# A delta-net scan kept in two halves of one PSUM bank, its output products in the attention's ring

## The chip, the cores and the metric

The kernel runs on one core of a Trainium2 chip. The metric is the device time of one execution in microseconds. Its engines are TensorE (PE, with its weight loads as PEld), VectorE (DVE), ScalarE (ACT), GpSimd (POOL) and SyncE (SP, which here only issues DMAs).

## The reference

Two layers act on 1280 tokens (256 of context, 1024 latent). Each layer normalises and modulates its input, multiplies it by one wide input weight, sends the parts through three branches, and adds the gated product with one output weight to the residual. A final norm follows. The branches are a gated delta net (GDN, 4 heads of 64), multi-head latent attention (8 heads), and gated linear attention (GLA, 4 heads). GDN and GLA are scanned in both directions, by chunks:

```
def step(state, xs):                       # gated delta net, one chunk of 64
    v_new = ui - wi @ state
    o = (qi * exp(gi)) @ state + ai @ v_new
    state = state * exp(g_last) + (ki * exp(g_last - gi)).T @ v_new
```

The GLA scan has the same form without the first line: `o = (qi * exp(bi)) @ state + scores @ vi` and a decayed state plus `k.T @ v`. The output is the normed latent stream, 1024 x 1024 in float32. The second layer needs no output for context tokens.

## The kernel before

A layer runs in stages that `run` (L1419) strings together: input projections and convolution, preparation of the delta net's triangular inverses, the up-projection of attention (`up`), attention itself (`attend`), and the output projection (`proj_start`, `proj`). Beside `up` and `attend` runs a **background**, a Python generator that gives out instructions piece by piece: the delta net's scan (`gdn_scan`, L683), then the GLA preparation and its seven levels, then the GLA scan (`gla_scan`, L926). After each unit of `up` the background gets three turns, until 28 have been taken in all (`UPS`); after each piece of `attend` it gets one turn. What is left when attention has been given out is drained, and then comes `proj_start`.

This order of the program gives the priorities. At compile time a planner simulates the engines, and of the instructions that are ready in its simulation it places the one that comes first in the program; each engine then runs its list strictly in the order so made. A lower instruction can thus stand ahead of a higher one that was not ready.

PSUM has eight banks of 128 x 512 float32. One (`tag="l"`, one buffer) belongs to the background for the whole of `up` and `attend`. The other seven are the ring "u" during `up`; during `attend` they are two score tiles `sa` of two banks each, one bank `sb`, and the ring "t" of **two** banks, from which attention takes one tile for each group of four transposes of the probabilities (`ptr`, L1243, copied out at L1247) and one for each output (`O`, L1255 to L1271). A new tile of a ring waits until every access of the tile that it replaces is over. Two engines' accesses to one bank are kept apart even where they touch different columns.

**One step of the delta net's scan** (20 in a layer, both directions and four heads at once; `S` is the state) takes three tiles of bank "l" in turn:

- `kS` (L730): the key products with S into columns 0 to 255 and, where the step has an output, the query products into 256 to 511. DVE forms `r` from the left half (L732, L733) and `qs` from the right (L736). Then a turn ends.
- `Tr` (L740): the products of the triangular inverse with `r`; DVE makes `vn` (L742). A turn ends.
- `F` (L748, L759): the state's product in the left half, which DVE adds to the decayed state to make the next S (`Sg`, L754; the decay `sd` is POOL's, L753); and the intra-chunk product of `at` with `vn` in the right half, which DVE adds to `qs` to give the output `oS` (L762). After steps 3, 15 and 19 POOL adds the two directions (L774) and `head_norm` gates them and stores them. A turn ends.

In the first layer every step has an output, in the second those from step 4 on. All float32 matmuls count as two records in the trace.

**One step of the GLA scan** (10) takes three tiles of the same bank: `kdt` (L950, two transposes of keys, copied by ACT to `ktl` at L952), `gO` (L961, L964: products with the state and with the scores, taken out by L973 or L975) and `gF` (L980, from which DVE makes the next state, L982 and L988). Each of the three ends a turn.

`proj_start` (L1296) loads attention's results (`yst`, L1316), splits the first output weights, makes gate rows (L1331, L1332) and turns the gated GDN and GLA results (`ytr`, L1350, from `yx`, L1346). Its SBUF pool is opened when the background's pools have been closed. `proj` goes on with `ytr` and the products `po` (L255 to L257).

Of the kernel before, what the change touches and what calls it, by code (L numbers as in the profile page):

```python
# [43 lines left out]
class Net:  # L44
# [638 lines left out]
    def gdn_scan(self, l):  # L683
# [8 lines left out]
        S = None  # L692
# [7 lines left out]

        for s in range(20):
# [3 lines left out]
            def kq(m, d, h):  # L705
                return self.KQ[h % 2].rearrange("q (m p i t) -> q m p i t", m=2, p=2, t=64)[R[d], m, h // 2, cc[d] // 2]
# [5 lines left out]
            def be(m):  # L712
# [13 lines left out]
            if S is not None:  # L726
                pk = self.g("kS", "l")
                for m in range(2 if out else 1):
                    for d, h in lanes:
                        mm(pk[R[d], 256 * m + 64 * h:256 * m + 64 * h + 64], kq(m, d, h), S[R[d], hs(h)], start=True, stop=True)  # L730
                r = sp.tile([128, 256], F32, name="r", tag="r", bufs=1)
                V.tensor_tensor(v3(r), v3(pk[:, 0:256]), be(3), ALU.mult)  # L732
                V.tensor_tensor(r, vt, r, ALU.subtract)  # L733
                if out:
                    qs = sp.tile([128, 256], F32, name="qs", tag="qs", bufs=1)
                    V.tensor_tensor(v3(qs), v3(pk[:, 256:512]), be(3), ALU.mult)  # L736
                yield
            pt = self.g("Tr", "l")
            for d, h in lanes:
                mm(pt[R[d], hs(h)], ci(self.TT, d, h), r[R[d], hs(h)], start=True, stop=True)  # L740
            vn = sp.tile([128, 256], F32, name="vn", tag="vn", bufs=1)
            V.tensor_tensor(v3(vn), v3(pt[:, 0:256]), be(0), ALU.mult)  # L742
            yield
            pf = self.g("F", "l")
            if s < 19:
                P.tensor_tensor(v3(kt), v3(kt), be(1), ALU.mult)
                for d, h in lanes:
                    mm(pf[R[1 - d], hs(h)], kt[R[d], hs(h)], vn[R[d], hs(h)], start=True, stop=True)  # L748
                Sn = sp.tile([128, 256], F32, name="Sg", tag="Sg", bufs=2)
                if S is not None:  # L750
# [3 lines left out]
                    V.tensor_tensor(Sn, sd, pf[:, 0:256], ALU.add)  # L754
                else:
                    V.tensor_copy(Sn, pf[:, 0:256])
            if out:
                for d, h in lanes:
                    mm(pf[R[d], 256 + 64 * h:256 + 64 * h + 64], at[R[d], h % 2, 64 * (h // 2):64 * (h // 2) + 64], vn[R[d], hs(h)], start=True, stop=True)  # L759
                o = oS[:, 256 * s:256 * s + 256]  # L760
                if S is not None:
                    V.tensor_tensor(o, qs, pf[:, 256:512], ALU.add)  # L762
                else:
                    V.tensor_copy(o, pf[:, 256:512])
            S = Sn
            for j in {3: (0,), 15: (2, 3), 19: (1, 4)}.get(s, ()):
# [817 lines left out]
```

## Time and profile before

| | |
|---|---|
| three runs, median (lowest to highest) | 2283.36 us (2278.01 to 2290.98) |
| the profiled execution's own time | 2280.18 us |
| its span, first to last instruction | 2278.4 us |
| PE busy | 2043.3 us, 90% |
| PE weight loads busy | 1709.8 us, 75% |
| DVE / ACT / POOL busy | 1291.6 (57%) / 941.1 (41%) / 743.7 (33%) us |
| mean granted TensorE clock | 0.946 |

Stages by time in the profile: the first layer's up-projection with the scan 499 to 618 us, a joint with little PE work to 646, attention with the scan to 781, with the GLA levels to 954, with the GLA scan to 1052, attention's rest to 1076, then the output projection. In the second layer the scan beside attention lasts from 1773 to 1907, the GLA scan from 2043 to 2137, attention's rest to 2171.

How to read it: a row names the engine, the line of the kernel, the operation, and out<-in by tile. In the timeline `[x <-y]` after a row is idle time of that engine just before it and what ended it. A row of a stage gives its bounds and length, then busy us and instructions of PE, PEld, DVE, ACT and POOL, then the granted share of TensorE's full clock, the busy share of the DMA engines and GB/s. Busy time of PE includes the overlap of pipelined matmuls, so a busy PE is not PE at its peak.

### The profile page before, as it was taken

How to read it: one execution, taken by the hardware profiler on the slowest of the kernel's cores; microseconds unless marked ns; L12 is line 12 of the kernel's file. 1: busy time of each engine (PE TensorE's matmuls, PEld its weight loads, DVE VectorE, ACT ScalarE, POOL GpSimd, SP SyncE). 2: the span in 40 equal slices, each digit the busy share in tenths (PEclk: the TensorE clock that was granted, in tenths of full speed). 3: DMA queues.
4: the chain of work that ended last, by engine and by line, in shares of the span. 5: the costliest groups of instructions: out<-in, count | busy, mean ns of one | idle time of the engine just before them, and what ended most of it. 6: DMA issues, size and time to landing. Idle time of an engine off the chain costs nothing.

```text
span 2278.4 us, 44490 instructions
## 1 busy us (share of the span) xinstructions
PE 2043.3 (90%) x17820; PEld 1709.8 (75%) x17820; DVE 1291.6 (57%) x2187; ACT 941.1 (41%) x1926; POOL 743.7 (33%) x936
## 2 busy tenths in 40 slices
PE   5998997999989988898897998976987999899998
PEld 3987896886767766676897987875876776667688
DVE  3446685323447689656425356795233677975634
ACT  3246311533235466555204356212542445564531
POOL 1233265122234543214103322381123264421410
PEclk8999998899989999999898999998998999899999
DMA  7111343258742231113424212424266242101352
GB/s 296 47 62 61 105 119 113 84 200 284 220 109 76 76 111 36 40 48 121 161 93 171 65 36 81 136 69 115 90 197 168 58 115 96 54 24 50 100 155 103
DMA packets 207551, 247.34 MB, mean 109 GB/s; under 512 B 60976, under 2 KB 164464, under 8 KB 203760
## 3 DMA queue, kind: packets, MB, share of 16 engines
q1 hardware_dynamic: 207344, 244.49, 34.1%
q8 instruction: 140, 2.29, 0.4%
q14 instruction: 67, 0.55, 0.1%
HBM read 168.14 MB, written 76.28 MB: 107 GB/s over the span
## 4 chain that ended last, share of the span: by engine, by line
PE 46%; DVE 13%; ACT 5%; DMA 5%; issue 3%; POOL 2%; SPq 1%; DVEq 0%; POOLq 0%; ACTq 0%
PE O L1255 6%; PE ptr L1243 4%; PE po L257 3%; PE po L255 3%; PE po L256 3%; PE sa L255 3%; PE sa L256 2%; PE sa L257 2%; PE ptk L255 1%; PE ptk L256 1%; PE ptk L257 1%; DVE XT L634 1%; DVE X L636 1%; PE kS L730 1%; DVE acc L345 1%
## 5 line engine op out<-in xcount | busy, mean ns | idle before, releaser
L255 PE MATMUL ptk<-whi,hhi 128*128 128x256 f32 (+1 forms) x912 | 263.6, 290 | 6.1 <-DVE ev L297 2.2
L257 PE MATMUL ptk<-whi,hlo 128*128 128x256 f32 (+1 forms) x912 | 261.9, 288 | 1.8 <-POOL hlo L238 1.7
L256 PE MATMUL ptk<-wlo,hhi 128*128 128x256 f32 (+1 forms) x912 | 261.7, 287 | 0.4 <-DVE wlo L250 0.4
L1243 PE MATMUL ptr<-c_id,P 128*128 128x128 f32 x1312 | 203.6, 283 | 27.8 <-ACT PT L1247 18.8
L1243 PEld LDWEIGHTS ptr<-c_id,P 128*128 128x128 f32 x1312 | 151.2, 143 | 78.1 <-ACT PT L1247 29.9
L1247 ACT COPY PT<-ptr 128x512 f32<-128x512 f32 (+1 forms) x256 | 122.3, 480 | 211.1 <-PE ptr L1243 209.7
L256 PE MATMUL pin<-hlo,whi 128*128 128x512 f32 (+1 forms) x544 | 201.6, 371 | 1.6 <-issue 1.6
L255 PE MATMUL pin<-hhi,whi 128*128 128x512 f32 (+1 forms) x544 | 202.5, 372 | 0.0
L257 PE MATMUL pin<-hhi,wlo 128*128 128x512 f32 (+1 forms) x544 | 201.8, 372 | 0.0
L255 PEld LDWEIGHTS ptk<-whi,hhi 128*128 128x128 f32 x912 | 179.4, 197 | 10.8 <-issue 4.3
L1206 DVE TENSOR_REDUCE mx<-sa 128x1 f32<-128x1024 f32 x128 | 156.2, 1220 | 53.6 <-PE sa L257 53.0
L257 PEld LDWEIGHTS ptk<-whi,hlo 128*128 128x128 f32 x912 | 178.8, 197 | 5.3 <-POOL hlo L238 3.0
L256 PEld LDWEIGHTS ptk<-wlo,hhi 128*128 128x128 f32 x912 | 179.4, 197 | 3.1 <-issue 2.0
L1255 PE MATMUL O<-PT,vv 128*64 128x256 f32 x1312 | 169.6, 388 | 1.7 <-ACT PT L1247 0.9
L255 PE MATMUL po<-wohi,yh 128*128 128x256 f32 x576 | 164.4, 286 | 4.4 <-DVE yl L1353 2.1
L256 PE MATMUL po<-wolo,yh 128*128 128x256 f32 x576 | 164.0, 285 | 0.0
L257 PE MATMUL po<-wohi,yl 128*128 128x256 f32 x576 | 162.6, 285 | 0.0
L1228 ACT ACTIVATE P<-sa,mx 128x1024 f32<-128x1024 f32 x128 | 142.2, 1111 | 0.0
L1255 PEld LDWEIGHTS O<-PT,vv 128*64 128x64 f32 x1312 | 97.2, 138 | 59.0 <-issue 11.9
L255 PE MATMUL sa<-kTh,qTh 128*128 128x512 f32 (+1 forms) x272 | 118.3, 436 | 21.1 <-ACT kTh L1152 15.2
L250 POOL TENSOR_TENSOR wlo<-wst,whi 128x1024 fp32r<-128x1024 f32 x32 | 84.1, 2639 | 127.5 <-ACT whi L249 126.4
L256 PEld LDWEIGHTS pin<-hlo,whi 128*128 128x128 f32 x544 | 105.6, 194 | 19.7 <-issue 4.4
(341 smaller groups left out, 5030.6 us busy)
## 6 DMA issues: line engine op xcount, KB each, us to landing
wada<-in_w_ada_dram SPq DMA_DIRECT2D x24, 1024.0 KB
wst<-in_w_in_dram SPq DMA_DIRECT2D x48, 512.0 KB
kv<-ktv_d SPq DMA_DIRECT2D x80, 128.0 KB
wost<-in_w_out_dram SPq DMA_DIRECT2D x16, 512.0 KB
xt<-in_x_all_dram SPq DMA_DIRECT2D x10, 512.0 KB
at_d<-D SPq DMA_DIRECT2D x4, 1280.0 KB
kn_d<-uo SPq DMA_DIRECT2D x20, 256.0 KB
v_d<-uo SPq DMA_DIRECT2D x20, 256.0 KB
```

The costliest lines, as they stand in the source:

```text
L250: E.tensor_tensor(lo[:, h], st, hi[:, h].bitcast(F32), ALU.subtract)
L255: mm(out, lh, rh, start=first, stop=False)
L256: mm(out, lh, rl, start=False, stop=False)
L257: mm(out, ll, rh, start=False, stop=last)
L345: nc.vector.scalar_tensor_tensor(a, raw[:, tap:tap + 1282], cw[:, ti, tap:tap + 1], a, ALU.mult, ALU.add)
L634: E.tensor_tensor(tmp, Xv[B, G, 0:k, k].unsqueeze(3).broadcast_to([q, n, nr, ncl]), Xv[B, G, k, k + 1:32].unsqueeze(2).broadcast_to([q, n, ...
L636: E.tensor_tensor(dst, dst, tmp, ALU.add)
L1206: V.tensor_reduce(mx[:, 0:1], sas[u], AX.X, ALU.max, negate=True)
L1228: A.activation(p[:, 0:1024], ta, AF.Exp, bias=mx[:, 0:1], accum_out=r[:, 0:1])
L1243: nc.tensor.transpose(tp[:, 128 * (k - ka):128 * (k - ka) + 128], p[:, 128 * c:128 * c + 128], self.ident)
L1247: (V.tensor_copy if ka == 4 else A.copy)(PT[hh][:, ka:kb, 128 * (i % 2):128 * (i % 2) + 128], tp[:, 0:128 * (kb - ka)].rearrange("p (k t) ...
L1255: mm(po[64 * h2:64 * h2 + 64, 0:256], vv[m][:, 128 * k + 64 * h2:128 * k + 64 * h2 + 64], PT[h2][:, k, :], start=(k == 0), stop=(k == nk - 1))
```

## The change

The scan holds one tile `W` of bank "l" for all its steps. `pa` is its left half, `pb` its right half. Key products go to `pa`, the triangular products to `pb`, the state's products to `pa` again. The query products and the `at` products are put into a closure, `pending`, which is called in the next step, behind that step's key products, with a turn of its own (the last step calls it at once). It takes a tile from ring "u" while `up` runs and from ring "t" in `attend`: query products in the left half, `at` products in the right. `qs` and the output addition follow there, and then `gather`, which holds what the step did before at its end. `vn` has two buffers instead of one.

In the GLA scan one tile `W` of bank "l" serves all key transposes, in alternating halves; `gO` and `gF` come from ring "t".

```diff
--- before.py
+++ after.py
@@ -689,7 +689,9 @@
         V, A, P = nc.vector, nc.scalar, nc.gpsimd
         bev = self.bev
         oS = sp.tile([128, 20 * 256], F32, name="oS", tag="oS", bufs=1)
-        S = None
+        W = self.g("scan", "l")
+        pa, pb = W[:, 0:256], W[:, 256:512]
+        S = pending = None
         lanes = [(d, h) for h in range(4) for d in range(2)]
 
         def hs(h):
@@ -697,19 +699,33 @@
 
         def v3(t):
             return t.rearrange("q (h t) -> q h t", t=64)
+
+        def gather(s):
+
+            for j in {3: (0,), 15: (2, 3), 19: (1, 4)}.get(s, ()):
+                if last and j == 0:
+                    continue
+                o = sp.tile([128, 512], F32, name="oG", tag="oG", bufs=2)
+                for i in range(2 * j, 2 * j + 2):
+                    for e in range(2):
+                        c, R = 2 * i + e, slice(64 * e, 64 * e + 64)
+                        b = 3 - c if c < 4 else 23 - c
+                        P.tensor_tensor(o[R, 256 * (i % 2):256 * (i % 2) + 256], oS[R, 256 * c:256 * c + 256],
+                                        oS[R, 256 * b:256 * b + 256], ALU.add)
+                self.head_norm(l, 0, o, j)
 
         for s in range(20):
             cc = (s, 3 - s if s < 4 else 23 - s)
             R = [slice(64 * (c % 2), 64 * (c % 2) + 64) for c in cc]
 
-            def kq(m, d, h):
+            def kq(m, d, h, R=R, cc=cc):
                 return self.KQ[h % 2].rearrange("q (m p i t) -> q m p i t", m=2, p=2, t=64)[R[d], m, h // 2, cc[d] // 2]
 
             def ci(t, d, h):
                 o = 128 * (cc[d] // 2) + 64 * (h // 2)
                 return t[d, h % 2][R[d], o:o + 64]
 
-            def be(m):
+            def be(m, s=s):
                 return bev[:, s, m].rearrange("q p h -> q (p h)").unsqueeze(2).broadcast_to([128, 4, 64])
 
             kv = sp.tile([128, 512], F32, name="kv", tag="kv", bufs=KVB)
@@ -724,56 +740,55 @@
                     nc.sync.dma_start(at[R[d]], self.at_d[l][:, R[d], o:o + 128].rearrange("h q t -> q h t"))
             r = vt
             if S is not None:
-                pk = self.g("kS", "l")
-                for m in range(2 if out else 1):
-                    for d, h in lanes:
-                        mm(pk[R[d], 256 * m + 64 * h:256 * m + 64 * h + 64], kq(m, d, h), S[R[d], hs(h)], start=True, stop=True)
+                for d, h in lanes:
+                    mm(pa[R[d], hs(h)], kq(0, d, h), S[R[d], hs(h)], start=True, stop=True)
                 r = sp.tile([128, 256], F32, name="r", tag="r", bufs=1)
-                V.tensor_tensor(v3(r), v3(pk[:, 0:256]), be(3), ALU.mult)
+                V.tensor_tensor(v3(r), v3(pa), be(3), ALU.mult)
                 V.tensor_tensor(r, vt, r, ALU.subtract)
-                if out:
-                    qs = sp.tile([128, 256], F32, name="qs", tag="qs", bufs=1)
-                    V.tensor_tensor(v3(qs), v3(pk[:, 256:512]), be(3), ALU.mult)
                 yield
-            pt = self.g("Tr", "l")
+            if pending:
+                pending()
+                yield
             for d, h in lanes:
-                mm(pt[R[d], hs(h)], ci(self.TT, d, h), r[R[d], hs(h)], start=True, stop=True)
-            vn = sp.tile([128, 256], F32, name="vn", tag="vn", bufs=1)
-            V.tensor_tensor(v3(vn), v3(pt[:, 0:256]), be(0), ALU.mult)
+                mm(pb[R[d], hs(h)], ci(self.TT, d, h), r[R[d], hs(h)], start=True, stop=True)
+            vn = sp.tile([128, 256], F32, name="vn", tag="vn", bufs=2)
+            V.tensor_tensor(v3(vn), v3(pb), be(0), ALU.mult)
             yield
-            pf = self.g("F", "l")
+            Sn = None
             if s < 19:
                 P.tensor_tensor(v3(kt), v3(kt), be(1), ALU.mult)
                 for d, h in lanes:
-                    mm(pf[R[1 - d], hs(h)], kt[R[d], hs(h)], vn[R[d], hs(h)], start=True, stop=True)
+                    mm(pa[R[1 - d], hs(h)], kt[R[d], hs(h)], vn[R[d], hs(h)], start=True, stop=True)
                 Sn = sp.tile([128, 256], F32, name="Sg", tag="Sg", bufs=2)
                 if S is not None:
                     sd = sp.tile([128, 256], F32, name="sd", tag="sd", bufs=1)
                     for d in range(2):
                         P.tensor_tensor(v3(sd[R[1 - d]]), v3(S[R[d]]), be(2)[R[d]], ALU.mult)
-                    V.tensor_tensor(Sn, sd, pf[:, 0:256], ALU.add)
+                    V.tensor_tensor(Sn, sd, pa, ALU.add)
                 else:
-                    V.tensor_copy(Sn, pf[:, 0:256])
+                    V.tensor_copy(Sn, pa)
+            pending = None
             if out:
-                for d, h in lanes:
-                    mm(pf[R[d], 256 + 64 * h:256 + 64 * h + 64], at[R[d], h % 2, 64 * (h // 2):64 * (h // 2) + 64], vn[R[d], hs(h)], start=True, stop=True)
-                o = oS[:, 256 * s:256 * s + 256]
-                if S is not None:
-                    V.tensor_tensor(o, qs, pf[:, 256:512], ALU.add)
-                else:
-                    V.tensor_copy(o, pf[:, 256:512])
+                def pending(s=s, R=R, S=S, vn=vn, at=at, kq=kq, be=be):
+
+                    po = self.g("F", "u" if "u" in self.psb else "t")
+                    if S is not None:
+                        for d, h in lanes:
+                            mm(po[R[d], hs(h)], kq(1, d, h), S[R[d], hs(h)], start=True, stop=True)
+                    for d, h in lanes:
+                        mm(po[R[d], 256 + 64 * h:256 + 64 * h + 64], at[R[d], h % 2, 64 * (h // 2):64 * (h // 2) + 64],
+                           vn[R[d], hs(h)], start=True, stop=True)
+                    o = oS[:, 256 * s:256 * s + 256]
+                    if S is not None:
+                        qs = sp.tile([128, 256], F32, name="qs", tag="qs", bufs=1)
+                        V.tensor_tensor(v3(qs), v3(po[:, 0:256]), be(3), ALU.mult)
+                        V.tensor_tensor(o, qs, po[:, 256:512], ALU.add)
+                    else:
+                        V.tensor_copy(o, po[:, 256:512])
+                    gather(s)
             S = Sn
-            for j in {3: (0,), 15: (2, 3), 19: (1, 4)}.get(s, ()):
-                if last and j == 0:
-                    continue
-                o = sp.tile([128, 512], F32, name="oG", tag="oG", bufs=2)
-                for i in range(2 * j, 2 * j + 2):
-                    for e in range(2):
-                        c, R = 2 * i + e, slice(64 * e, 64 * e + 64)
-                        b = 3 - c if c < 4 else 23 - c
-                        P.tensor_tensor(o[R, 256 * (i % 2):256 * (i % 2) + 256], oS[R, 256 * c:256 * c + 256],
-                                        oS[R, 256 * b:256 * b + 256], ALU.add)
-                self.head_norm(l, 0, o, j)
+            if s == 19:
+                pending()
             yield
 
 
@@ -937,6 +952,7 @@
         oL = [self.bp.tile([128, 512], F32, name="oL", tag="oL", bufs=5) for _ in range(5)]
         order = (tuple(range(10)), (1, 0) + tuple(range(9, 1, -1)))
         S = [None, None]
+        W = self.g("kdt", "l")
         for st in range(10):
             vs, kt = [], None
             for d in range(2):
@@ -944,16 +960,16 @@
                 nc.sync.dma_start(vv, self.gv_d[l][order[d][st]])
                 vs.append(vv)
             if st < 9:
-                pk = self.g("kdt", "l")
+                pk = W[:, 256 * (st % 2):256 * (st % 2) + 256]
                 for d in range(2):
                     i = order[d][st]
                     nc.tensor.transpose(pk[:, 128 * d:128 * d + 128], K[d][:, 128 * i:128 * i + 128], self.ident)
                 kt = sp.tile([128, 256], F32, name="ktl", tag="ktl", bufs=2)
-                A.copy(kt, pk[:, 0:256])
+                A.copy(kt, pk)
                 yield
             todo = [d for d in range(2) if not (last and order[d][st] < CT) and (d == 0 or S[d] is not None)]
             if todo:
-                ps = self.g("gO", "l")
+                ps = self.g("gO", "t")
                 for d in todo:
                     i = order[d][st]
                     pd = ps[:, 256 * d:256 * d + 256]
@@ -975,7 +991,7 @@
                         V.tensor_tensor(o, pd, o, ALU.add)
                 yield
             if st < 9:
-                pf = self.g("gF", "l")
+                pf = self.g("gF", "t")
                 for d in range(2):
                     mm(pf[:, 256 * d:256 * d + 256], kt[:, 128 * d:128 * d + 128], vs[d], start=True, stop=True)
                 Sn = sp.tile([128, 512], F32, name="Sl", tag="Sl", bufs=2)
```

## Rows read from the trace of the kernel before

**Rows 1.** Stages: length, busy by engine (instructions), granted clock, DMA share, GB/s.

```profile
646.00:781.00 135.00, 133.36 (x1458) 101.92 (x1458) 90.34 (x183) 66.72 (x159) 53.29 (x76) 1.00 0.26 74
...
954.00:1052.00 98.00, 94.89 (x617) 74.80 (x616) 63.44 (x125) 49.65 (x127) 23.88 (x31) 1.00 0.18 55
1052.00:1076.00 24.00, 21.56 (x148) 13.25 (x147) 14.59 (x37) 12.82 (x27) 13.18 (x13) 1.00 0.43 136
1076.00:1091.00 15.00, 6.01 (x27) 4.58 (x26) 3.31 (x7) 7.83 (x15) 9.14 (x6) 0.65 0.86 289
...
1773.00:1907.00 134.00, 133.58 (x1526) 104.29 (x1525) 93.30 (x188) 63.55 (x149) 52.54 (x75) 1.00 0.27 75
...
2137.00:2171.00 34.00, 29.47 (x204) 20.37 (x203) 19.26 (x44) 22.01 (x48) 20.33 (x20) 1.00 0.43 134
```

**Rows 2.** Timeline, PE, two scan steps of layer two: start us, us, instruction.

```profile
1804.61 1.15 PE L730 MATMUL kS<-Sg,KQ 64*64 64x64 f32 x32
...
1807.94 0.68 PE L740 MATMUL Tr<-r,TT 64*64 64x64 f32 x16
...
1809.48 0.68 PE L748 MATMUL F<-vn,kv 64*64 64x64 f32 x16
...
1813.88 1.15 PE L730 MATMUL kS<-Sg,KQ 64*64 64x64 f32 x32
...
1819.51 0.68 PE L740 MATMUL Tr<-r,TT 64*64 64x64 f32 x16
...
1823.79 0.68 PE L748 MATMUL F<-vn,kv 64*64 64x64 f32 x16
...
1828.64 1.15 PE L730 MATMUL kS<-Sg,KQ 64*64 64x64 f32 x32
```

**Rows 3.** Timeline, DVE, the query operation in the first of these steps.

```profile
1806.15 0.41 DVE L736 TENSOR_TENSOR qs<-kS,bes 128x256 f32<-128x256 f32 x1
```

**Rows 4.** Timeline, PE, layer one: key products of steps 10 and 19.

```profile
646.02 1.36 PE L730 MATMUL kS<-Sg,KQ 64*64 64x64 f32 x24
...
770.93 1.15 PE L730 MATMUL kS<-Sg,KQ 64*64 64x64 f32 x32
```

**Rows 5.** Timeline, PE, a scan step in the joint of layer one.

```profile
619.27 1.15 PE L730 MATMUL kS<-Sg,KQ 64*64 64x64 f32 x32 [1.15 <-DVE oS L762]
...
626.15 1.97 PE L730 MATMUL kS<-Sg,KQ 64*64 64x64 f32 x32 [0.52 <-DVE oS L762]
```

**Rows 6.** Timeline, SyncE, the background's last stores and the next issues, both layers.

```profile
1061.85 0.36 SPq L1009 DMA_DIRECT2D y_d<-oL  x1
1062.26 0.95 SPq L1316 DMA_DIRECT2D yst<-yT_d  x2
...
2147.07 2.37 SPq L1009 DMA_DIRECT2D y_d<-oL  x2
2149.49 0.95 SPq L1316 DMA_DIRECT2D yst<-yT_d  x2
```

**Rows 7.** Timeline, PE, from attention's end to the first projection product, layer one.

```profile
1075.88 0.60 PE L1350 MATMUL ytr<-c_id,yx 128*128 128x128 f32 x4
...
1080.69 0.69 PE L1350 MATMUL ytr<-c_id,yx 128*128 128x128 f32 x2 [4.21 <-ACT gate L1332]
...
1090.43 0.56 PE L255 MATMUL po<-wohi,yh 128*128 128x256 f32 x1
```

**Rows 8.** Timeline, PE, first and last of nine key transposes, GLA scan, layer one.

```profile
954.15 0.38 PE L950 MATMUL kdt<-c_id,KK 128*128 128x128 f32 x2
...
1038.62 0.44 PE L950 MATMUL kdt<-c_id,KK 128*128 128x128 f32 x2
```

**Rows 9.** Tile ptr in attention, layer one: copies, then who waited (us, times).

```profile
L1247 ACT COPY PT<-ptr x128: 354/480/625, 655.8 to 1070.2; 128x512 f32<-128x512 f32 x64, 128x256 f32<-128x256 f32 x64
L1247 DVE COPY PT<-ptr x64: 653/681/693, 658.6 to 1066.9; 128x512 f32<-128x512 f32 x64
...
  PE ptr L1243: 9.5, 17
```

## The prediction

> **What bounds the kernel now.** I read the busy shares first (the table above): TensorE (PE) leads with 90% of the span, so a change of order can win no more than PE's gaps. Next I cut the span by stage to see where they lie [rows 1]. While the delta net's scan runs beside attention (646 to 781 us, and 1773 to 1907 in the second layer), PE idles 1.6 us of 135 and 0.4 us of 134 at full clock: there the scan is filler. Between the two scans lie the GLA levels, which the change does not touch. Beside the GLA scan 3.1 us of 98 are idle; in the attention's last stretch alone 2.4 of 24 and 4.5 of 34; in the opening of the output projection (1076 to 1091) 9.0 of 15, at a mean granted clock of 0.65.
>
> Third view, the steps of the scan [rows 2, 3]: first key products (kS), Tr, F, the next kS. They come in pairs of 9.3 and 14.8 us, 12.0 on average; in the first layer nine steps take 124.9 us, 13.9 each [rows 4]. Free of other work a step takes 6.9 us, and there the wait before it has a name: oS before kS, 1.15 us [rows 5]. So the background is bound by its own latency, while the time beside it is bound by PE.
>
> Fourth view, SyncE's queue [rows 6]: the projection's first loads (yst) leave 0.4 us after the background's last store (1061.85, then 1062.26; in the second layer 2147.07 and 2149.49). Its pool takes the background's SBUF, so the end of the background, not that of attention, starts the projection's preparation. In the first layer this comes too late: from 1075.88, with attention over, until the first projection product at 1090.43, PE mostly waits, longest for a gate copy (4.21 us) [rows 7]. That is where a faster background could pay.
>
> **The change part by part.** *Instructions.* No product and no eviction is added or taken away; kS's 32 PE records become 16 now and 16 in the later closure, and gathers follow their outputs. Neither queue gets another DMA. Loads of kv and at are issued where they were; at and vn are held about a step longer (at has three buffers, vn two). Cost 0; cover for a late release is the step's own length, and if it were gone one at load, some 2 us, would stand on the output product alone, not on the chain.
>
> *The scan's chain loses* half of kS (1.15/2 = 0.58 us) and the qs operation (0.41 us, rather 0.33 as they overlap) between kS and Tr: 0.9 us. From F to the next kS there now stand the output product, its DVE addition and the bank's release: 4.40 and 4.85 us, mean 4.6 [rows 2]. What is left has the shape of Tr to F (PE, one DVE operation, PE): 1.54 and 4.28, mean 2.9. So it loses 1.7 there, 2.6 us a step in all. Bounds: 0 (PE puts other work in between), and 4.0 (always the short 1.54). The moved products (16 + 16 records, about 1.2 us) lie while DVE forms r, before Tr; on the chain they could cost up to 1.2. I take 2.6, nearest to the mean legs.
>
> *More yields.* A step with an output yields four times instead of three, and the up-projection gives the background 28 steps. Before, these reach through Tr of step 9 (2 for step 0, then 3 each); after, to the outputs of step 6 in the first layer, and of step 7 in the second, where steps 0 to 3 have none. So about two steps and one step move out of the up-projection and the joint into attention, where PE is full: at 1.15 + 3 x 0.68 = 3.2 us of PE each up to 9.6 us, against which the up-projection shortens by as much as it was PE-bound. Bounds -3 and +10; I take +2, as the joint still lets PE host a step or two at 6.9 us [rows 5].
>
> *End of the scan.* First layer: 11 steps of 11.3 us from 646 instead of 135 us, 11 us earlier; second: 11.5 steps of 9.4 instead of 134, 26 us earlier.
>
> *GLA scan.* Nine key transposes start 10.56 us apart (954.15 to 1038.62 in eight steps) [rows 8]. With kdt alone in the bank and gO and gF in the ring, the only chain is F, Sl, Sl, gO; it needs two visits to PE, 2 x 2.9 us at the leg measured above, but the ring and program order hold it: between 5.8 and 10.56 I take 8. Nine times 2.5: 23 us earlier in each layer. Background's end together: some 34 and 49 us earlier; at the bounds 0 and 80.
>
> *What that buys.* The first layer's opening lasts 14.55 us [rows 7], its preparation begins 13.6 us before attention's end. With 34 us more, gates, casts and the first turned tiles are ready; a last reload of yx stays. Gain 12, bounds 0 and 16 (the products after 1090.43 run at the half clock at first). Second layer: preparation already starts 21 us ahead; of the 4.5 us idle [rows 1] I take 2.5, bounds 0 and 4.5.
>
> *What it costs.* Attention left alone idles 10% (2.4 of 24), beside the GLA scan 3%: 34 us x 7% + 49 us x 7% = +6, bounds 0 and 10.
>
> *The ring.* "t" has two buffers and serves ptr and O. The change adds 13 + 12 output products, and gO and gF 19 + 17: 61 tiles. Behind a PE instruction that waits for a slot stand the chain's Tr and the attention's transposes and scores, since PE is in order; the copies on ACT and DVE wait for those. In the first layer's attention 192 ptr tiles were copied, and PE waited for ring or copies 9.5 us in 17 waits [rows 9]: 0.05 us a tile, or 0.56 if every tile waits. That is +3 to +34; I take +3, since most slots are free when asked for and the compile-time order puts other ready work ahead of a full ring.
>
> *Sum* against the profiled execution (2280.2 us, span 2278.4 and 1.8 around it): -12 - 2.5 + 6 + 3 + 2 = -3.5, so **2277 us**. The three runs have a median of 2283.4, so my base lies 3.2 us under it, which is less than can be told apart: I count within 0.5% (11.4 us, 2272 to 2294.8) as the same.
>
> **The rivals.**
>
> *B, the ring binds.* If a tile on the ring costs 0.4 us instead of 0.05, 61 x 0.4 = 24 us stand against the gain: 2280.2 + 24 + 6 + 2 - 14.5 = **2298**, slower. It decides from 0.35 us a tile. For it: O holds its slot for a whole run of 40 records and two DVE operations, so ptr already shares one slot then, and each output product or gO is held through one or two DVE operations of 0.4 us in a busy queue. Against it: 0.05 so far [rows 9]. The Trainium skill ("Perfetto Trace Analysis", Optimization Strategy) says that the same gap recurring on the engine that should be full can mean too few PSUM buffers for the next tile. No such gap recurs in this trace's scan stretches, 1.6 and 0.4 us idle; three users on two slots would be the place to see it.
>
> *C, all of it is won.* The background ends 40 us or more earlier, the opening vanishes (-14.5), the second layer's idle 4.5 goes too, the tail idles no more than before because the projection's preparation fills it: 2280 - 19 - 1 for the half clock = **2260**. For it: yst follows the last store at once in both layers. Against it: attention alone had gaps of 10 to 13%.
>
> *D, it does not do what it says.* The legs of 4 to 6 us hold attention work that PE had at hand, such as the run of O products in every second step; a chain that is ready earlier may only find other work ahead of it, and the end stays where it is: **2280**.
>
> **How the numbers follow.** Forecast 0.42 (own range 2268 to 2289), B 0.22, C 0.26, D 0.10. Faster than 2272: nearly all of C and a quarter of the forecast's, 0.36. Slower than 2294.8: most of B and a little of the forecast's, 0.21. The same: 0.43. The range for 8 in 10 reaches into B and C: 2257 to 2300.
>
> **What would show it.** Right: scan steps near 9 to 11 us in attention, no wait of kS for oS; the background's last store 30 to 50 us before attention's end instead of 13 and 22; a gap of under 4 us between the last O product and the first projection product in the first layer; PE waits for ring slots (ptr, F, gO, gF) together under 15 us. Wrong: steps still of 12 to 14 us (D); PE idle over 6% beside the scan or the GLA scan, on waits for PT copies, Sl or oL (B); or a tail as full as the scan (C). The sum itself is wrong if the joint between up-projection and attention (618 to 646) grows by more than 5 us, since I hold it bound by loads and left it out.

## The result and the profile after

The changed kernel takes **2413.8 us** (median of 4 runs, 2406.1 to 2421.5) against 2283.3 for the kernel before beside it: ratio 1.057, 95% interval 1.052 to 1.062. It is slower, far outside my range of 2257 to 2300. Its profiled execution took 2406.1 us, with a span of 2404.2, 125.8 more than before. The layers share the loss: the first projection product of layer one starts at 1155.5 us instead of 1090.4 [rows 7], 65 us later, and the remaining 61 arise behind it.

The slices of the page (40 equal parts of 60 us; busy tenths of PE, then its granted clock) show two dents that the kernel before does not have, one in each layer's attention:

```profile
PE   5998988999686499999997998968997746899998
PEclk7999998999897599999998999989998957999999
```

The busy time by stretch (bounds, length, then busy us and instructions of PE, PEld, DVE, ACT, POOL, granted clock, DMA share, GB/s) puts layer one's dent between 750 and 850 us. After:

```profile
600.00:650.00 50.00, 33.07 (x414) 29.19 (x413) 15.38 (x40) 9.87 (x19) 16.74 (x21) 0.83 0.58 156
650.00:750.00 100.00, 86.24 (x1199) 66.37 (x1198) 69.74 (x141) 43.33 (x99) 55.15 (x70) 0.98 0.36 108
750.00:850.00 100.00, 51.39 (x586) 35.37 (x584) 69.41 (x126) 36.27 (x80) 29.21 (x41) 0.54 0.04 12
...
900.00:1000.00 100.00, 93.11 (x614) 67.68 (x611) 63.43 (x119) 61.50 (x143) 34.97 (x42) 1.00 0.32 94
```

And the kernel before, in stretches that its rows above do not have:

```profile
600.00:650.00 50.00, 36.20 (x431) 31.44 (x431) 15.57 (x36) 10.48 (x21) 19.73 (x21) 0.80 0.60 164
650.00:750.00 100.00, 99.59 (x1084) 76.33 (x1083) 68.81 (x142) 50.55 (x119) 44.26 (x62) 1.00 0.27 75
750.00:850.00 100.00, 89.36 (x908) 65.42 (x908) 76.77 (x133) 59.76 (x136) 48.88 (x56) 0.95 0.31 94
...
900.00:1000.00 100.00, 91.87 (x622) 67.10 (x621) 67.41 (x127) 60.15 (x148) 26.69 (x38) 0.98 0.16 47
```

Over 650 to 850 us PE does 137.6 us of work instead of 189.0, and from 750 to 850 it does so at a mean granted clock of 0.54, near the lower of TensorE's two levels. Behind the dent PE is as busy as before (93.1 of 100 us from 900 to 1000, before 91.9), but there is much more of attention left. What happens at the two edges of the dent, PE's timeline tells:

```profile
741.29 0.38 PE L1259 MATMUL ptr<-c_id,P 128*128 128x128 f32 x2
742.29 1.08 PE L889 MATMUL gsc<-qx,KK 128*32 128x128 f32 x32 [0.62 <-issue]
...
750.03 0.40 PE L257 MATMUL sa<-kTh,qTl 128*128 128x512 f32 x1
...
839.93 0.69 PE L966 MATMUL kdt<-c_id,KK 128*128 128x128 f32 x2 [1.39 <-ACT A L911]
841.07 2.08 PE L996 MATMUL gF<-gvt,ktl 128*128 128x256 f32 x4 [0.46 <-ACT ktl L968]
842.94 1.06 PE L1259 MATMUL ptr<-c_id,P 128*128 128x128 f32 x4
```

The last `ptr` before the dent starts at 741.29, the next at 842.94, right behind the first `gF` of the GLA scan. Between them PE gets GLA products (`gsc`) and, up to 750.03, the last of the scores that had been begun. From then until `gF` is out, over 90 us, PE runs nothing of attention, the work that should fill it. The waits of PE over the whole program (us in all, times, longest) look harmless beside that:

```profile
...
PE gsc L889 <- ACT A L900: 20.6, 3, 8.0
...
PE ptr L1259 <- ACT PT L1263: 18.0, 35, 2.3
...
PE scan L753 <- DVE r L747: 16.0, 17, 5.5
...
PE ptr L1259 <- DVE PT L1263: 14.1, 32, 1.1
...
```

The same two waits of `ptr` in the kernel before:

```profile
PE ptr L1243 <- ACT PT L1247: 18.8, 24, 3.9
...
PE ptr L1243 <- DVE PT L1247: 4.7, 8, 1.6
```

None of these waits comes near the length of a dent. In the dent PE waits for GLA's own operands, since the list made at compile time holds nothing else for it there. The background, with the engines to itself, ends early: its last store and the projection's first load on SyncE were at 1061.85 and 1062.26 [rows 6], now

```profile
902.44 0.48 SPq L1025 DMA_DIRECT2D y_d<-oL  x1
...
904.17 1.06 SPq L1332 DMA_DIRECT2D yst<-yT_d  x2
```

Layer one's opening, from the last output of attention to the first `po`, has shrunk, as forecast, from 14.55 us [rows 7] to 7.9:

```profile
1147.63 1.53 PE L1366 MATMUL ytr<-c_id,yx 128*128 128x128 f32 x12
1153.92 1.94 PE L1366 MATMUL ytr<-c_id,yx 128*128 128x128 f32 x8 [4.76 <-DMA yx<-y_d]
1155.51 0.56 PE L255 MATMUL po<-wohi,yh 128*128 128x256 f32 x1
```

### The profile page after: what moved, and what is told of

The parts are those of the page before. It is cut to its first block, busy times and chain, and to the rows that moved or that the text cites. A ratio compares the mean times of both kernels' runs of the same rounds, so it can differ in the third digit from the quotient of the medians.

```text
span 2404.2 us, 44533 instructions
## 1 busy us (share of the span) xinstructions
PE 2058.3 (86%) x17820; PEld 1716.6 (71%) x17820; DVE 1291.0 (54%) x2187; ACT 942.2 (39%) x1926; POOL 742.0 (31%) x936
## 4 chain that ended last, share of the span: by engine, by line
PE 43%; DVE 13%; ACT 5%; DMA 4%; issue 4%; POOL 3%; SPq 1%; DVEq 0%; POOLq 0%; ACTq 0%
PE O L1271 6%; PE ptr L1259 5%; PE po L255 3%; PE po L256 3%; PE po L257 3%; PE sa L255 2%; PE sa L256 2%; PE sa L257 2%; PE ptk L255 2%; PE ptk L256 2%; PE ptk L257 2%; PE gsc L889 1%; DVE XT L634 1%; DVE acc L345 1%; DVE X L636 1%
## 5 line engine op out<-in xcount | busy, mean ns | idle before, releaser
L1271 PE MATMUL O<-PT,vv 128*64 128x256 f32 x1312 | 152.5, 382 | 0.7 <-ACT PT L1263 0.5
L1271 PEld LDWEIGHTS O<-PT,vv 128*64 128x64 f32 x1312 | 91.5, 137 | 51.2 <-issue 6.2
```

The costliest lines, as they stand in the source:

```text
L1271: mm(po[64 * h2:64 * h2 + 64, 0:256], vv[m][:, 128 * k + 64 * h2:128 * k + 64 * h2 + 64], PT[h2][:, k, :], start=(k == 0), stop=(k == nk - 1))
```

## The experiments

Theory 1: a ring gives out its slots in **program order**. The background's new tiles stand early in the program but are reached late, and attention's later tiles must wait for them. Theory 2 is my rival B: two slots are too few for 61 more tiles, each dear. Theory 3: the scan's halves and its added turns cost the time.

### One tile of the ring in each layer

```
 (kernel before, gla_scan)
-                pf = self.g("gF", "l")
+                pf = self.g("gF", "l" if st else "t")
```

> The kernel before, with one thing changed: of all background tiles only the gF of the first GLA step of each layer is taken from the attention's ring t instead of bank l (one tile a layer, two in the whole kernel). Theory 1 (program order): the ring gives its two slots out in program order; the one gF stands about 59 turns into the attention's 450 (398 in the second layer), while the background reaches it only at about 960 us. So no second ptr tile behind it can be placed, and attention must stop some 60 us after it begins until the GLA levels are through: PE under 60% busy over at least 80 us in each layer, first gF well before 960 us, total at least +60 us (over 2340). Theory 2 (two slots are too few for 61 more tiles, each dear): two tiles at 130/61 = 2.1 us are 4 us, total 2280 to 2290, no hole. Theory 3 (the scan's halves and its turns cost the time): 2283, no hole.

Measured: 2468.3 us, ratio **1.081** (1.078 to 1.085). Two tiles in the whole kernel cost 186 us, more than the 61 of the change. Its timeline on PE:

```profile
697.25 0.40 PE L257 MATMUL sa<-kTh,qTl 128*128 128x512 f32 x1
...
699.29 0.68 PE L748 MATMUL F<-vn,kv 64*64 64x64 f32 x16 [1.04 <-DVE vn L742]
...
716.99 1.97 PE L730 MATMUL kS<-Sg,KQ 64*64 64x64 f32 x32 [0.52 <-DVE oS L762]
...
863.34 2.02 PE L980 MATMUL gF<-gvt,ktl 128*128 128x256 f32 x4
865.15 1.06 PE L1243 MATMUL ptr<-c_id,P 128*128 128x128 f32 x4
```

The last scores before the stop start at 697 us. Then PE gets the background's products alone, the scan's and behind them the GLA's, until `gF` at 863.34; the first `ptr` follows at 865.15. The place fits the count of turns: attention's transposes begin at 639.9 us, it took some 435 us for its 450 turns before, the tile stands some 59 turns into them, and 59 turns at 0.97 us lead, by this estimate, to 697. Busy time by stretch:

```profile
650.00:750.00 100.00, 77.03 (x970) 61.56 (x972) 53.97 (x115) 26.32 (x64) 35.76 (x52) 0.78 0.19 54
750.00:850.00 100.00, 39.23 (x594) 27.84 (x592) 64.21 (x119) 37.93 (x78) 37.63 (x46) 0.52 0.12 43
```

Theory 1 is shown, and a price per tile (theory 2: 4 us) is out. That it costs more than the whole change fits the same order: attention reaches the tile while the scan is still under way (last state at 742.6 us, shown further down), and stands still for the rest of the scan too.

### Each half of the change alone

```
 scan only:  gdn_scan as changed;  gla_scan as before (kdt, gO, gF in "l")
 GLA only:   gdn_scan as before;   gla_scan as changed (gO, gF in "t")
```

> The changed delta net scan (chain in two halves, output products in t), with the GLA scan as it was before (kdt, gO, gF in bank l). Theory 1 (program order): no background tile of the ring stands behind the GLA levels, so the stretch 750 to 850 us is full again (PE over 85 of 100 us instead of 51); what is left of the loss is the scan's own stretch, 650 to 750, where PE had 86 of 100 us instead of 99.6, about 13 us a layer, against an earlier end of the background: total 2275 to 2315. Theory 2 (slots too few for the number of tiles, 25 of 61 left): 2283 + 130 x 25/61 = 2336. Theory 3 (the halves and turns of the scan): nearly all of the loss stays, 2395 or more.

> The delta net scan as it was before (four tiles a step in bank l), with the changed GLA scan (kdt in halves of bank l, gO and gF in t). Theory 1 (program order): attention must wait at the first gO until scan and GLA levels are through; as the old scan has no output tile to hold attention beside it, attention reaches that place early and the hole is at least as long as in the changed kernel: PE under 60% over 80 us or more in each layer, total 2370 to 2450. Theory 2 (number of tiles, 36 of 61): 2283 + 130 x 36/61 = 2360, spread over the GLA scan, with no hole before it. Theory 3 (the scan's halves): 2283.

Measured: scan only 2310.1 us, ratio 1.012 (1.008 to 1.016), as theory 1 had it; GLA only 2488.6, ratio 1.090 (1.086 to 1.093), still longer than I had said. First scan only, then GLA only:

```profile
650.00:750.00 100.00, 88.30 (x1210) 67.92 (x1208) 68.81 (x142) 41.71 (x94) 56.66 (x71) 0.96 0.34 105
750.00:850.00 100.00, 83.67 (x868) 60.31 (x867) 89.25 (x157) 60.58 (x140) 38.91 (x49) 0.90 0.17 46
```

```profile
650.00:750.00 100.00, 79.02 (x959) 63.20 (x957) 52.60 (x111) 26.89 (x64) 35.45 (x53) 0.76 0.20 59
750.00:850.00 100.00, 40.27 (x627) 29.71 (x624) 64.00 (x120) 36.33 (x75) 37.30 (x46) 0.50 0.12 43
```

Without GLA tiles in the ring the dent is all but gone (83.7 of 100 us, where I had expected over 85 and the kernel before has 89.4), and 28 us are left, with PE at 88.3 instead of 99.6 from 650 to 750: I read it as the small form of the same coupling, beside the scan. With GLA's tiles and no others, the dent begins earlier, as in the run with one tile. The two parts do not add up (28 and 207 against 131), because the stop is shorter in the changed kernel: from the last scores to the first `ptr` behind it, it lasts there from 750 to 843 us, and with GLA's tiles alone from 700 to 868. Its background comes to the first `gF` sooner (841 against 867 us), and its attention comes to the stop later. For that, two causes are at hand and not told apart: the scan's own tiles hold attention, and the scan's 19 added turns move the first `gO` from turn 59 to 78.

### A ring of its own for the background, and the price of a slot

```
-                self.ps, self.psb = self.pool(st, "psB", space=PSUM), {"t": 2}
+                self.ps, self.psb = self.pool(st, "psB", space=PSUM), {"t": 1, "b": 1}
 (own ring: the changed kernel, with the scan's output products, gO and gF in "b")
 (control: the kernel before, with {"t": 1})
```

> The changed kernel, with the two banks of the attention's ring divided: one slot t for ptr and O, one slot b of their own for the background's output products, gO and gF. Theory 1 (program order): no attention tile stands behind a background tile any more, so the holes of 750 to 850 us and its like in the second layer are gone (PE over 80 of 100 us); what it costs is the one slot fewer for ptr and O, which no row shows (bounds 0 and 0.6 us for each of some 350 tiles, 200 us); I take 40 us, total 2320, and a loss spread evenly over attention. Theory 2 (too few slots): worse than the changed kernel, over 2414, as attention has half of the slots; a hole has no reason to go. Theory 3: no change against 2414 beside the price of the slot.

> The kernel before, with one slot instead of two in the attention's ring t; the background keeps bank l and no tile of it is in the ring. It prices a missing slot alone. If the division of the ring took the whole hole away and its 2605 us are only the price of the slot, this kernel lies within 40 us of it: 2560 to 2610, with PE near 37 of 50 us through the whole of attention, on waits of ptr for the PT copies. If a coupling to the background was still left in the divided ring, this kernel is much faster than that: under 2500.

Measured: 2605.3 us, ratio 1.141 (1.138 to 1.144), and for the control 2572.9, ratio 1.128 (1.126 to 1.131). Own ring, then control:

```profile
750.00:850.00 100.00, 75.31 (x833) 52.90 (x832) 84.25 (x151) 57.70 (x130) 37.89 (x51) 0.83 0.22 65
1050.00:1100.00 50.00, 35.84 (x196) 24.70 (x192) 17.68 (x33) 19.32 (x43) 13.54 (x14) 0.86 0.16 45
```

```profile
750.00:850.00 100.00, 77.51 (x814) 54.79 (x815) 72.69 (x128) 51.37 (x113) 44.77 (x54) 0.85 0.23 72
1050.00:1100.00 50.00, 35.93 (x167) 24.80 (x167) 15.01 (x27) 18.01 (x44) 11.63 (x12) 0.77 0.10 30
```

My 40 us for the missing slot were far off: alone it costs 292 us, which is 0.68 us for each of the 428 tiles that attention takes from the ring (392 copies of `ptr`, 36 outputs). Taken alone, the own ring would have spoken for theory 2. Beside its control it is 32 us slower, and in 750 to 850 it has no dent that the control does not have (75.3 and 77.5). So capacity is precious for attention's own turnover, but the change took no slot away, and with the ring divided its dent is gone: the missing slot is not what the change lost.

### The same tiles at later places in the program

```
-                for _ in self.attend(l):
-                    if bg is not None and next(bg, bg) is bg:
+                for turn, _ in enumerate(self.attend(l)):
+                    if turn % 4 == 0 and bg is not None and next(bg, bg) is bg:
 ...
 (paced: the changed kernel; control: the kernel before;
  late: everything ahead of the GLA scan over 80% of attention's turns, the GLA scan over the next 18%)
```

> The changed kernel with its two slots and all its 61 tiles, but in attention the background gets one turn for every fourth turn of attention instead of every one. Its ring tiles so stand over the whole of attention in program order (turns 4 to 420 of 450) instead of in its first quarter. Theory 1 (program order): the places come near to the times at which the background gets there, the hole of 750 to 850 us is gone (PE over 80 of 100), most of the 130 us come back: 2270 to 2320. Theory 2 (too few slots for so many tiles): as many tiles in as many slots, so 2390 to 2430. Theory 3 (the scan's halves): 2414 or slightly more.

> The control to the paced version: the kernel before, the background again with one turn for every fourth of attention. No tile of the background stands in the ring, so by theory 1 program order acts here only as the rank of the background's work, and the time stays near the kernel before: 2270 to 2310. If the pace itself were worth something whatever the ring, this kernel gains or loses as much as the paced version of the changed kernel does: if that comes back by over 90 us, this one would come out at 2200 or less.

> The changed kernel with a background whose turns are laid out to the times at which the kernel before got there: everything ahead of the GLA scan over the first 80% of attention's turns, the GLA scan over the last 18%. In the version with every fourth turn the first gO stood at 68% (first layer) and attention still overtook it (900 to 1000 us had PE at 67 of 100). By program order the remaining stand shortens with the distance: 2280 to 2320, clearly under the 2348 of every fourth turn, with PE over 80 of 100 in each 100 us of attention. If what is left there is the price of 61 more tiles in two slots, it stays at 2340 to 2360.

Measured: paced 2347.7 us, ratio 1.030 (1.028 to 1.032); control 2276.5, ratio 0.999 (0.997 to 1.001); late 2368.0, ratio 1.039 (1.035 to 1.042). Paced, then late:

```profile
900.00:1000.00 100.00, 66.79 (x590) 46.92 (x588) 67.08 (x130) 49.11 (x115) 28.02 (x43) 0.81 0.08 23
```

```profile
900.00:1000.00 100.00, 81.20 (x825) 56.82 (x823) 88.45 (x160) 57.98 (x135) 42.20 (x52) 0.90 0.09 26
1100.00:1150.00 50.00, 28.97 (x149) 19.79 (x148) 23.21 (x42) 21.82 (x39) 25.99 (x19) 0.73 0.64 203
```

With the same tiles in the same two slots, half of the loss goes, and the control shows that the pace itself is worth nothing where no tile is shared. The dent has moved to 900 to 1000 us (66.8), where attention reaches the first `gO`: with every fourth turn that stands at turn 308, by the estimate above (0.97 us a turn from 644.6 us) at 943 us, and the last scores before the stop start at 940. That speaks for program order again; but my 2270 to 2320 was too low, and the late version, above both of the ranges that I gave for it, refuted the simple form of the theory. Its first `gF` came at 1019 us instead of 982, and much of its loss is in the opening (29.0 of 50 us in 1100 to 1150). I read it so: a later place does not only free attention, it holds the background. The kernel before was not run with the late layout, so what the layout costs without a shared ring is not shown; the next runs test the reading at a fixed pace.

### The halves without the ring, and the scan's pace

```
 (halves: the kernel before; one tile W = pa | pb of bank "l" for the whole scan)
-                pk = self.g("kS", "l")      kS: key products in pa, query products in pb
-            pt = self.g("Tr", "l")          Tr in pb
-            pf = self.g("F", "l")           state's products in pa, output products in pb
 (scan only, paced: turn % 2, turn % 3, turn % 4 as above)
```

> The kernel before, whose scan keeps one bank-l tile for all steps and divides it: kS's key part, F and the state's sums in one half, Tr and the output product in the other (the query part of kS there too, before Tr). Same yields, nothing in the ring. So it is the halves by themselves, without the ring. By the terms of my forecast a step loses part of what it waits for (up to 1.7 us of 12, as kS no longer waits for the output's addition): the background ends 15 to 35 us earlier and the total is 2268 to 2280. By the rival that a background which ends earlier is worth nothing, because attention then runs alone with 8 to 10% idle: 2280 to 2300. If the halves themselves cost the 130 us: 2395 or more.

> The changed delta net scan with the GLA scan as before, and one background turn for every fourth turn of attention. It asks where the 28 us of the scan-only kernel come from. If from the places of the 25 output tiles in the ring (they stand in the first tenth of attention's turns, while the scan takes over 100 us of it), spreading them brings most of it back: 2275 to 2292, with PE over 97 of 100 us in 650 to 750 instead of 88. If from attention running alone for longer once the background has ended 50 us earlier, with no coupling, it stays within 2300 to 2320, as nothing is done about the idle 8 to 10% there.

> Changed delta net scan, old GLA scan, one background turn for every second turn of attention. With every turn the ring held attention (PE 88 of 100 us from 650 to 750, scan's last state at 721 us, 2310); with every fourth it held the scan (PE 97.5 of 100, last state at 794 instead of 767 us, preparation of the projection late, 2334). If the ring simply ties the two streams to each other's places, there is an even place between: last output product at turn 62 of 450, near 706 us, last state between 721 and 767, total 2275 to 2300 and under both. If a ring shared with the scan costs its 20 to 50 us wherever the tiles stand, this is 2305 to 2340.

> The same with one background turn for every third turn of attention: last output product at turn 93 of 450, near 735 us. If the ring ties the two streams to each other's places: last state between 740 and 775 us, PE over 95 of 100 us from 650 to 750, total 2280 to 2310, between every second and every fourth turn. If a shared ring costs the same wherever the tiles stand: 2305 to 2340.

Halves: 2279.9 us, ratio 0.999 (0.998 to 1.000). So the halves by themselves cost nothing, which ends that part of theory 3. The time lies at the edge of what I gave to my forecast's terms, but by luck: the scan is no faster. The time at which the scan's states (`Sg`) are through shows what each version does to it (duration ns lowest/median/highest, first and last start in the stretch); before, halves, scan only, scan only with every fourth turn, then the kernel before with every fourth turn and with one tile in the ring:

```profile
L754 DVE TENSOR_TENSOR Sg<-sd,F x12: 406/420/422, 615.5 to 767.3; 128x256 f32<-128x256 f32 x12
```

```profile
L753 DVE TENSOR_TENSOR Sg<-sd,scan x12: 406/420/422, 613.6 to 766.8; 128x256 f32<-128x256 f32 x12
```

```profile
L767 DVE TENSOR_TENSOR Sg<-sd,scan x13: 409/420/422, 604.8 to 721.4; 128x256 f32<-128x256 f32 x13
```

```profile
L767 DVE TENSOR_TENSOR Sg<-sd,scan x12: 404/410/422, 617.2 to 794.1; 128x256 f32<-128x256 f32 x12
```

```profile
L754 DVE TENSOR_TENSOR Sg<-sd,F x12: 407/420/422, 614.0 to 768.4; 128x256 f32<-128x256 f32 x12
```

```profile
L754 DVE TENSOR_TENSOR Sg<-sd,F x12: 408/420/422, 615.1 to 742.6; 128x256 f32<-128x256 f32 x12
```

The halves by themselves leave the scan where it was (766.8 against 767.3): `kS` still has its 32 records with the query products in the other half, and still waits for `oS` (1.15 us at 617 us, as in [rows 5]). The scan is 46 us earlier with the output products out of the bank; but attention is held beside it there, and the old scan too comes 25 us earlier (742.6) where attention stands still. How much of the 46 us is the shorter chain is therefore open. With every fourth turn the scan is later than before (794.1), although its chain is the short one. The pace is not the cause: at the same pace, with no tile shared, the last state is at 768.4. What is left is that the scan's output products must wait for the attention tiles ahead of them in the ring. With every fourth turn, as expected, attention was full; the loss reappeared in the opening, which I had not counted:

```profile
650.00:750.00 100.00, 97.50 (x1028) 73.80 (x1027) 62.95 (x127) 47.83 (x116) 33.01 (x50) 1.00 0.24 67
1050.00:1100.00 50.00, 24.02 (x148) 16.32 (x145) 25.91 (x50) 14.77 (x26) 20.99 (x17) 0.79 0.47 147
```

It took 2334.1 us (1.023, 1.021 to 1.025), outside what I expected by either reason. The projection's first load leaves at 1091.2 us; at the same pace with no shared tile it left at 1063.2, so the background as a whole is held. Every second turn gave 2298.5 (1.007, 1.005 to 1.009), just inside what I expected of a ring that ties both streams, with the last state at 754.3 us. Every third gave 2310.7 (1.012, 1.010 to 1.014): by the time that is just above the range of such a ring (2280 to 2310) and inside the range of a fixed price of the shared ring (2305 to 2340), while the last state, at 773.8, lies where the tie puts it. Every turn had given 2310.1. The order of the last states with the pace (721, 754, 774, 794) speaks for the tie; the times by themselves do not decide. Every second, then every third:

```profile
650.00:750.00 100.00, 95.69 (x1176) 73.97 (x1177) 67.57 (x138) 41.24 (x98) 46.23 (x63) 0.96 0.28 78
1050.00:1100.00 50.00, 41.58 (x297) 29.79 (x296) 26.13 (x53) 29.28 (x67) 17.07 (x18) 0.99 0.34 100
```

```profile
650.00:750.00 100.00, 97.79 (x1116) 74.52 (x1114) 65.70 (x132) 46.56 (x110) 38.36 (x56) 0.99 0.28 76
1050.00:1100.00 50.00, 37.86 (x239) 26.77 (x237) 28.08 (x61) 24.58 (x55) 21.16 (x21) 0.92 0.33 104
```

What attention wins from 650 to 750 (88.3, 95.7, 97.8, 97.5 of 100 with every, every second, third and fourth turn) PE loses from 1050 on, as the background ends later (43.9, 41.6, 37.9, 24.0 of 50; the projection's first load leaves at 1008, 1043, 1073 and 1091 us). The best of these paces is every second turn, and even there the shared ring is 0.7% slower than the kernel before. No version with a shared ring beats it.

## Why the prediction was wrong

The step that failed is "**The ring** ... I take +3, since most slots are free when asked for and the compile-time order puts other ready work ahead of a full ring". The runs showed in its place a stop of over 90 us in layer one, set by one tile's place in the program. The cost is not in the number of tiles, so my bounds of 0.05 and 0.56 us a tile bounded the wrong quantity [rows 9]: those are waits among tiles of one stream. The new tiles belong to a stream that runs behind its place in the program. I had all that it takes to see this and did not put it side by side. The background has one turn for each of attention's, 28 of its 114 pieces are taken ahead, so in the kernel before the first `gO` stands some 59 turns into 450, at 13% (in the changed kernel, with its added turns, 78, at 17%), while [rows 8] have its transposes at 954 us, at 72% of the time from 640 to 1076. Over a bank of its own that lag was free. And of "other ready work" there is little: by the code a unit's scores need a buffer of probabilities that the `ptr` of an earlier unit frees, and in the timelines the scores stop with `ptr`, within 9 us.

Rival B pointed to the right place, with a price worked out by the same wrong unit: 24 us for 61 tiles, where two tiles cost 186. I weighed the Trainium skill ("Perfetto Trace Analysis", Optimization Strategy), that a recurring gap can mean too few PSUM buffers for the next tile. By its words one would look for a gap that repeats. This trace has none of that kind: attention is absent once in each layer, for some 92 and 83 us (750 to 843 and 1928 to 2011). The control with one slot shows what too few buffers look like in this kernel, PE at 36 of 50 us in the tail.

The other terms, one by one:

- **The scan's chain.** Forecast 11.3 us a step in layer one. In the changed kernel nine steps beside attention take 73.5 us (states at 644.68 and 718.15), 8.2 each; before it was 13.9 [rows 4]. The direction was right, but the size is not a test of the forecast, which was for a scan beside a full attention: here PE has 86.2 of 100 us from 650 to 750. Nearest to it is the version with every second turn, PE at 95.7, whose last state came 13 us earlier, where I had said 11. The halves alone gave nothing.
- **The background's end,** 34 and 49 us earlier. It came 158 and 76 us earlier (yst at 904.17 and 2073.84), the second although layer two began some 65 us later, and for another reason: attention stood still for it. With the scan alone it was 54 us earlier in layer one (1008.0).
- **The openings,** -12 and -2.5. Layer one won 6.7 in the changed kernel and 6.9 with the scan alone (7.6 us from 1096.33 to 1103.96): a reload of `yx` stays, which I had named, and PE waits 4.76 and 4.51 us for it. There the mechanism was right, the size half. In layer two the first `po` follows the last output at once (2303.10, 2303.63), but it did so before (2170.21, 2171.16), so hardly anything of the 2.5 is to be seen there.
- **Attention alone,** +6 for 83 us at 7%. The rate was near: from 2050 to 2300 PE has 227.7 of 250 us, 9% idle, where I had reckoned with 10%. The length was not: from the background's end to attention's it is 243 us in layer one and 229 in layer two, instead of 14 and 22 before.
- **Turns and the joint,** +2. In 600 to 650 PE has 33.1 us of work instead of 36.2, 3 us less, near the forecast; these rows do not show what that comes from.
- **What would show it.** I named PE's waits for the ring, under 15 us, as a sign that all is well. Those of `ptr` for PT copies are 32.1 us over the whole program (18.0 and 14.1) against 23.5 before (18.8 and 4.7): 9 us more, in a kernel that lost 126. The sign was blind: where lists are made ahead, a full ring shows as work that is absent. The other sign, PE over 6% idle beside the scan or the GLA, was the one that told, though not on the waits that I had named with it.

How far the 0.7% at the best pace comes from the coupling and how far from attention running alone is open, and so is the half of the loss that stays when the changed kernel is paced. A version in which the background keeps a bank of its own and attention keeps its two slots beside the moved products was not tried: the eight banks are all taken.

## What to carry to other kernels

Before you let two streams share a ring, compare where the guest's tiles stand in program order with when they are reached in time: a guest that lags stops its host about where its first unreached tile stands; one tile a layer was enough here. The tie holds in both directions, so moving the guest later delays it instead. Judge a stall in a kernel whose lists are made ahead by the work that is missing from a stretch, not by the waits that are recorded there.

## What the runs showed that I had not expected

Where the background has PE to itself, its steps become slower. With attention away, the granted clock from 750 to 850 us was 0.54 in the changed kernel and 0.52 with one tile; in the latter's timeline the 16 records of `F` take 0.68 us at 699 us, and those of `Tr` and `F` 1.12 from 712 on. A scan step from 708.72 to 716.99 takes 8.3 us, at a granted clock of 0.50 from 708 to 717, where the joint had 6.9 [rows 5] at 0.80 (619 to 626). As a whole the background still came sooner, as nothing stood in its way: `gF` at 863 us instead of 961. And one slot of a ring of two was worth 292 us, 13% of the kernel, though PE waited 9.5 us for that ring in the stretch that I had read [rows 9].
